# Modulation slices in staging tiles of their own, and 44 stores moved from SP to ACT, in a two-layer hybrid decoder trunk

## The chip, the core and the metric

The kernel runs on one core of a Trainium2 chip. The metric is device time in microseconds: the median over the runs of one kernel. Engines are named as the profile does: PE (TensorE, matrix products and transposes), PEld (its weight loads), DVE (VectorE), ACT (ScalarE), POOL (GpSimd) and SP (SyncE). SP computes nothing here; it is an in-order queue that starts DMA transfers. ACT starts some transfers too, between its own operations. An instruction that waits at the head of an engine's queue holds everything behind it.

## The reference

Two layers over 1024 tokens of width 1024, float32. Each layer:

```
mod = silu(c) @ w_mod + b_mod;  shift, scale, gate = split(mod, 3)
h = rms_norm(x, pre_gain) * (1 + scale) + shift
proj = h @ w_in                      # 1024 x 3088
A: sliding-window attention (window 128, 8 heads, 2 kv heads, rotary, sinks) * silu(ag)
B: rms_norm(retention(rq, rk, rv))  * silu(rg)       # 4 heads, chunks of 128 tokens
C: rms_norm(gated linear attention(gq, gk, gv, log_a)) * silu(gg)
y = concat(A, B, C) @ w_out
x = x + gate * rms_norm(y, post_gain)
```

The modulation is one row of 3 x 1024 values per layer, a product of a vector of 1024 with a 1024 x 3072 matrix.

## The kernel before

**Products.** Tokens are tiled by 128 (t = 0 to 7). A float32 product is made in three passes from a high part (rounded to the format that PE multiplies at full speed) and a low part (the rest). So every weight is loaded as float32, split into a high and a low part, and kept in an arena; activations are split in the same way.

**Weights.** A weight unit is 1024 x 256 (kv, aq0, rq, o0, ...). It comes in four loads of 256 KB (kc = 0 to 3, `issue`, L516), each into one tile of `stage()` (L119, tag `st`, 128 x 512, five buffers, BST). Four conversions (`conv`, L520) make the high parts (line L149 on ACT or L151 on DVE) and four the low parts (L533, three on DVE and one on POOL). A tile of the ring is free for a later load once the low part of its load has been made. The generator `loader` (L474) issues one load, converts one that is two loads old, and yields a delay (`ld1`, `ld2`).

**Modulation.** `mod_third` (L343) makes one third (j = 0 shift, 1 scale, 2 gate) of one layer's modulation in two halves (hh). A half has eight slices of w_mod, 256 KB each (L360), which DVE multiplies by the activated condition and adds up in `acc` (L362, L364). Every slice is put in a tile of `stage()`, the same ring of five as the weight units' loads. So is the row of post-norm gains (L376, L377). Of the 64 slices loaded this way, 16 belong to layer 0 and 48 to layer 1.

**Results of the heads.** Retention (`ret_core`, L1160) works on one token tile at a time: PE transposes the keys (L180), ACT copies them from PSUM (L149), PE makes the scores, DVE applies the causal mask (L1179), and so on; DVE updates the state (L1198, L1200). Gated attention (`gla_core`, L1078) has more steps on DVE, ACT and POOL (L1120, L1121 are its masked scores). `head_norm_gate` (L970) normalises a tile (square on ACT L973, sum on DVE L975, root on POOL L635, products on DVE L978, L979), transposes it, and calls `store_mix` (L954). That makes a high part (L149 on ACT) and a low part (L966 on DVE) and stores both in DRAM (mixS); in the last layer, for tiles 2 and up, a float32 copy as well (mixF). The projection with w_out reads them back.

**What sets the order.** PE's order is written out by hand: a projection emits its matmuls in pieces, and between pieces `pump` (L210) steps the other pieces of work that are due. Each is a generator (a job) that yields a delay from the table `L`, counted on a virtual clock `clk` that matmuls advance by their estimated cost (L164). So a delay decides behind which piece of a projection a small product of attention, retention or modulation stands. A key with `@1` is for layer 1. The order on DVE, ACT, POOL and SP comes from a scheduler that takes the program's instructions by their dependencies, so it moves when the program's order or its tiles move. The table `EN` names the engine of each optional step; `smh` is the store of high parts and of float32 copies, `sml` that of low parts, `lw` the weight loads, `lwm` the slices. `S` is SP and `A` ACT (`dma`, L153).

In the changed kernel all lines from L122 on stand 3 lower: L149 becomes L152, L154 becomes L157, L364 becomes L367.

Of the kernel before, what the change touches and what calls it, by code (L numbers as in the profile page):

```python
# [10 lines left out]
F32 = mybir.dt.float32  # L11
# [6 lines left out]
P = 128  # L18
D = 1024
S = 1024  # L20
# [73 lines left out]
def trunk(ctx: ExitStack, tc: tile.TileContext, ins, cst, out):  # L94
    nc = tc.nc
    V, A, G, T = nc.vector, nc.scalar, nc.gpsimd, nc.tensor
# [6 lines left out]
    gp = ctx.enter_context(tc.tile_pool(name="work", bufs=2))  # L103
# [5 lines left out]
    def nm(s):  # L109
        uid[0] += 1  # L110
        return f"{s}_{uid[0]}"
# [6 lines left out]

    def stage():  # L119
        return gp.tile([P, 512], F32, tag="st", name=nm("st"), bufs=BST)  # L120

    def small(w, dt=F32):  # L122
        return gp.tile([P, w], dt, tag="sm", name=nm("sm"), bufs=BS)
# [4 lines left out]
    def aux(dt=F32):  # L128
        return ps.tile([P, 512], dt, tag="aux", name=nm("aux"), bufs=8 - MMB)
# [14 lines left out]
    def eng(k):  # L144
        return G if EN[k] == "G" else V

    def copy(k, dst, src):
        if EN[k] == "A":
            A.activation(dst, src, AF.Copy)  # L149
        else:  # L150
            V.tensor_copy(dst, src)  # L151

    def dma(k, dst, src):  # L153
        {"S": nc.sync, "A": A, "P": G}[EN[k]].dma_start(dst, src)  # L154

# [8 lines left out]
    def mult(dst, lhsT, rhs, start, stop, cost=None):  # L164
        T.matmul(dst, lhsT, rhs, start=start, stop=stop)  # L165
        if cost is not None:
            clk[0] += cost
            return
        n = 1
        for d in rhs.shape[1:]:  # L170
            n *= d
        c = n / 2400.0
        if rhs.dtype == F32R:
            c = max(c, 0.107 if lhsT.shape[-1] > 64 else 0.055)
        else:
            c = max(4 * c, 0.21 if n > 2 else 0.03)
        clk[0] += c
# [5 lines left out]
    def lat(key, l):  # L183

        return L[key + "@1"] if l and key + "@1" in L else L[key]

# [3 lines left out]
    def flag(name, lat=0.0):  # L190
        flags[name] = clk[0] + lat
# [100 lines left out]
    def mod_tile(l, j):  # L292
        modc[(l, j)] = cp.tile([P, KT], F32, name=nm(f"mod{j}"), tag=f"mod{j}")
# [49 lines left out]
    def mod_third(l, j):  # L343
        if j < 2:
            mod_tile(l, j)
            rows = mod_rows(l, j)
            yield lat("mod1", l)
            rc = mod_rows_t(rows)
        else:
            res = cp.tile([P, D], F32, name=nm("modg"), tag="modg")  # L350
            modg[l] = res
        for hh in range(2):
            c0 = j * D + 512 * hh
            acc = gp.tile([P, 512], F32, tag="acc", name=nm("acc"), bufs=1)
            if j == 2:
                G.memset(acc, 0.0)
                nc.sync.dma_start(acc[0:1, :], b_mod[l:l + 1, c0:c0 + 512])
            for k in range(KT):
                wt = stage()
                dma("lwm", wt, w_mod[l, j, hh, :, k, :])  # L360
                if k == 0 and j < 2:
                    V.tensor_scalar(acc, wt, c_act[:, k:k + 1], None, ALU.mult)  # L362
                else:
                    V.scalar_tensor_tensor(acc, wt, c_act[:, k:k + 1], acc, ALU.mult, ALU.add)  # L364
                yield lat("mod2", l)
            yield lat("mod3", l)
            pm = aux()  # L367
            if j < 2:
                for b in range(4):
                    mult(pm[:, b:b + 1], acc[:, b * P:(b + 1) * P], ones[:, 0:1], True, True)  # L370
                mod_cols(l, j, hh, pm, rc)
                if j == 0:
                    flag(("modh", l, hh), lat("mod4", l))
            else:
                mult(pm, allones, acc, True, True)
                gain = stage()  # L376
# [216 lines left out]
    def sw_second():  # L593
        drain()
        for k in range(4):
# [7 lines left out]
            sw_split("T4", k, s4, "t4")  # L603
            yield L["sw1"]
        for name in ("T2", "T3", "T4"):
# [48 lines left out]
    def pre(l, t, xt, early=False, soon=False):  # L654
# [28 lines left out]
        for j in range(2):  # L683
# [33 lines left out]
    def pre_first(t):  # L717
        xt = [t2(), t2()]
        load_x(t, xt, nc.sync)
        yield L["pf3"] + L["pf2"] * (t - 4)  # L720
        yield from pre(0, t, xt)
# [950 lines left out]
        pump()  # L1672


B2, B1, BS, BST, MMB, SMB = 10, 8, 11, 5, 3, 3
EN = {"shw0": "V", "shw1": "A", "shw2": "A", "shw3": "A", "slw0": "V", "slw1": "G", "slw2": "V", "slw3": "G", "sht2": "A", "sht3": "A", "sht4": "A", "slt2": "V", "slt3": "G", "slt4": "G", "sd": "V", "mh0": "A", "mh1": "A", "mh2": "A", "mh3": "A", "mf": "A", "ms0": "V", "ms1": "V", "ms2": "V", "ms3": "V", "yg0": "V", "yg1": "V", "ml0": "V", "ml1": "V", "ml2": "V", "ml3": "V", "mod0": "A", "mod1": "V", "qst": "S", "smh": "S", "sml": "S", "sm0": "S", "sm1": "S", "lao": "S", "sao": "S", "lmix": "S", "ssg": "S", "lsg": "S", "ssr": "S", "lsr": "S", "lx": "S", "sx": "A", "lw": "S", "lwm": "S", "whi0": "V", "whi1": "A", "whi2": "A", "whi3": "A", "wlo0": "V", "wlo1": "V", "wlo2": "V", "wlo3": "G", "xn0": "V", "xn1": "V", "hlo0": "V", "hlo1": "V", "rot0": "V", "rot1": "V", "rdec": "V", "kslo": "V", "qslo": "V", "vlo": "G", "kT": "A", "qT": "A", "sprev": "A", "pn": "G", "pf0": "A", "aoc": "A", "hng": "V", "mh": "A", "gso": "V", "mg": "V", "mgl": "V", "rT": "A", "rv": "A", "gv": "A", "gk": "A", "ak0": "V", "ak1": "V", "ak2": "V", "ak3": "V", "kd0": "G", "kd1": "G", "kd2": "G", "kx1": "G", "kx2": "G", "kx3": "V", "kx4": "V", "qb": "G", "stx": "V"}
L = {"sw1": 0.4, "ld1": 1.2, "ld2": 1.2, "ld1@1": 1.2, "ld2@1": 1.27, "swW00": 0.0, "swT1": 0.0, "swW11": 0.4, "swW10": 0.5, "tt1": 8.0, "tt2": 1.75, "tb1": 24.5, "tb2": 0.75, "pf3": 13.2, "pf1": 6.35, "pf2": 4.16, "mod1": 4.6, "mod2": 4.0, "mod3": 13.29, "mod4": 7.04, "mod5": 3.36, "mod6": 9.04, "pre1": 7.44, "kv1": 3.1, "kv2": 2.11, "aq1": 6.0, "aq7": 6.0, "ag1": 5.44, "aq2": 2.4, "aq6": 5.2, "aq3": 10.21, "aq4": 7.36, "aq5": 3.6, "hn1": 8.93, "hn2": 2.85, "gz1": 11.18, "gz2": 8.13, "gl1": 2.76, "gd3": 15.9, "gc1": 0.62, "gc2": 1.94, "gc3": 1.33, "gc4": 0.87, "gc6": 0.86, "gc5": 1.14, "rc1": 0.8, "rc2": 1.09, "rc3": 5.87, "rc4": 2.51, "fin1": 7.28, "lay1": 1.13, "gc4@1": 0.93, "mod2@1": 4.0, "mod3@1": 15.1, "mod5@1": 3.36, "mod6@1": 4.11, "pre1@1": 7.44, "kv1@1": 2.79, "kv2@1": 5.28, "aq1@1": 4.8, "aq7@1": 5.28, "ag1@1": 6.25, "aq2@1": 0.82, "aq6@1": 6.0, "aq3@1": 10.9, "aq4@1": 4.4, "aq5@1": 5.15, "hn1@1": 8.12, "hn2@1": 2.85, "gz1@1": 15.91, "gz2@1": 10.94, "gl1@1": 4.6, "gd3@1": 15.9, "gc1@1": 0.48, "gc2@1": 1.94, "gc3@1": 1.33, "gc6@1": 0.86, "gc5@1": 1.04, "rc1@1": 0.37, "rc2@1": 0.84, "rc3@1": 1.9, "rc4@1": 2.79, "fin1@1": 4.28, "lay1@1": 1.7}
CHUNK = 7
LAG = 2
VDB = 8  # L1680
# [41 lines left out]
```

## Time and profile before

| | |
|---|---|
| median of 3 runs | 997.99 us (997.76 to 999.64) |
| the profiled execution | 996.31 us |
| its span | 994.6 us |
| mean granted clock of PE | 0.991 |
| PE busy | 965.7 us, 97% of the span |
| DVE, ACT, POOL busy | 683.2, 409.3, 246.3 us |
| share of PE in the chain that ended last | 80% |
| bytes moved | 148.77 MB |
| modulation slices | 64 loads of 256 KB, median 3.1 us to landing |
| unit loads from w_in | 96 loads of 256 KB, median 3.8 us to landing |

A row of instructions reads: start in us, duration in us, engine, line, operation, written tile <- read tile, shapes, and in brackets the idle time before it with what ended it. A row of waits reads: engine, tile and line of the waiting instruction, what it waited for, then total us, times, longest. A row of the chain reads: start, us, what the end of the kernel hung on at that time. `st` are tiles of the staging ring, `arena` the split weights, `acc` the sum of a modulation half, `t` and `mx` work tiles, `aux` and `mm` PSUM tiles, `SPq` and `ACTq` the engines' queues.

### The profile page before, as it was taken

What the parts mean: (1) busy time and instruction counts of PE and PEld (TensorE: products, weight loads), DVE (VectorE), ACT (ScalarE), POOL (GpSimd) and SP (SyncE); (2) the same over time, 40 slices, a digit from 0 to 9 for tenths busy, and PEclk for the clock granted to TensorE, in tenths of its full rate; (3) what the DMA queues carried; (4) which work ended last, traced back from release to release, by engine and by line L of the source; (5) the groups of instructions that cost most, each with busy time, mean ns of one, the idle gap of its engine ahead of it and who ended that gap; (6) DMA issues with size and microseconds to landing.
All of it is one profiled execution on the core that took longest, in us unless ns stands there. A gap on an engine that the chain in (4) does not pass through costs nothing.

```text
span 994.6 us, 19641 instructions
## 1 busy us (share of the span) xinstructions
PE 965.7 (97%) x7133; PEld 824.3 (83%) x7133; DVE 683.2 (69%) x1679; ACT 409.3 (41%) x1152; POOL 246.3 (25%) x310
## 2 busy tenths in 40 slices
PE   5899999999999999999999999999999999999996
PEld 1599999888998777778889999988999877777785
DVE  3779857677766777664677286775766577567876
ACT  2477312233332656632555332133333257574222
POOL 2322001233310234420124101113322034545000
PEclk8899999999999999999999999999999999999999
DMA  9843513523135355587555241352122434378883
GB/s 321 290 138 97 159 44 115 177 86 121 61 100 166 91 157 168 170 274 239 189 170 171 69 150 38 118 157 83 53 93 86 127 91 133 112 235 266 267 262 139
DMA packets 112305, 148.77 MB, mean 150 GB/s; under 512 B 12065, under 2 KB 63821, under 8 KB 112209
## 3 DMA queue, kind: packets, MB, share of 16 engines
q1 hardware_dynamic: 106512, 137.96, 44.5%
q10 hardware_dynamic: 5696, 9.56, 2.6%
q8 instruction: 56, 0.92, 0.4%
q14 instruction: 41, 0.33, 0.1%
HBM read 109.20 MB, written 36.18 MB: 146 GB/s over the span
## 4 chain that ended last, share of the span: by engine, by line
PE 80%; DVE 7%; DMA 7%; issue 2%; POOL 1%; ACT 1%; SPq 0%; ACTq 0%; POOLq 0%; DVEq 0%
PE mm L165 61%; PE aux L165 14%; PE aux L180 5%; DMA st<-in_w_in_dram 2%; POOL sm L635 1%; DMA t<-aoS 1%; DMA st<-in_w_last_dram 1%; DMA xk<-in_x_dram 1%; DVE arena L533 1%; DMA a<-mixS 1%; DVE t L1248 0%; DVE t L328 0%; DMA t<-in_x_dram 0%; DMA t<-xs 0%; DMA mixS<-t 0%
## 5 line engine op out<-in xcount | busy, mean ns | idle before, releaser
L165 PE MATMUL mm<-arena 128*128 128x256 f32 (+2 forms) x1824 | 299.9, 318 | 1.8 <-ACT arena L704 1.8
L165 PE MATMUL mm<-arena,arena 128*128 128x256 f32 (+2 forms) x1824 | 298.2, 316 | 0.0
L165 PEld LDWEIGHTS mm<-arena 128*128 128x128 f32 x1824 | 255.5, 191 | 26.0 <-issue 3.3
L165 PEld LDWEIGHTS mm<-arena,arena 128*128 128x128 f32 x1824 | 252.2, 188 | 24.3 <-issue 3.7
L635 POOL TENSOR_TENSOR sm<-sm,mhalf 128x1 f32<-128x1 f32 (+1 forms) x64 | 55.8, 872 | 335.9 <-DVE sm L634 317.8
L165 PE MATMUL mm<-arena,mx 128*128 128x512 f32 (+1 forms) x564 | 130.6, 387 | 0.5 <-ACT kept L1341 0.5
L165 PEld LDWEIGHTS mm<-arena,mx 128*128 128x128 f32 x564 | 101.4, 188 | 24.7 <-issue 1.9
L149 ACT ACTIVATE t<-aux 128x256 f32<-128x256 f32 (+2 forms) x124 | 55.8, 468 | 73.8 <-PE aux L180 62.2
L149 ACT ACTIVATE arena<-st 128x512 fp32r<-128x512 f32 x94 | 56.2, 627 | 53.2 <-DMA st<-in_w_in_dram 19.4
L929 POOL TENSOR_TENSOR smx<-smx,sm 128x512 f32<-128x512 f32 x32 | 36.1, 1129 | 125.7 <-DVE sm L928 118.0
L533 POOL TENSOR_TENSOR arena<-st,arena 128x512 fp32r<-128x512 f32 x31 | 42.7, 1378 | 79.7 <-ACT arena L149 72.9
L533 DVE TENSOR_TENSOR arena<-st,arena 128x512 fp32r<-128x512 f32 x77 | 58.0, 775 | 5.2 <-ACT arena L149 3.3
L925 ACT ACTIVATE smx<-smx,sm 128x129 f32<-128x129 f32 x128 | 49.9, 393 | 25.9 <-DVE sm L922 25.7
L364 DVE SCALAR_TENSOR_TENSOR acc<-st,c_act,acc 128x512 f32<-128x512 f32 x60 | 46.7, 778 | 16.9 <-DMA st<-in_w_mod_dram 16.5
L180 PE MATMUL aux<-c_ident,t 128*128 128x128 f32 (+1 forms) x292 | 48.2, 282 | 5.4 <-DVE t L666 5.0
L180 PEld LDWEIGHTS aux<-c_ident,t 128*128 128x128 f32 (+1 forms) x292 | 35.0, 144 | 12.4 <-DVE t L666 6.9
L698 ACT ACTIVATE t<-aux,mod,mod 128x128 f32<-128x128 f32 x68 | 25.9, 459 | 43.0 <-DVE t L1248 18.1
L165 PEld LDWEIGHTS aux<-t,mx 32*128 32x128 f32 (+1 forms) x896 | 39.5, 187 | 3.9 <-issue 2.1
L973 ACT ACTIVATE t<-aux 128x256 f32<-128x256 f32 x32 | 12.3, 383 | 73.6 <-PE aux L165 65.0
L165 PE MATMUL aux<-t,mx 32*128 32x32 f32 (+1 forms) x896 | 40.7, 272 | 0.0
L920 DVE COPY_PREDICATED smx<-c_curmask,aux 128x256 f32<-128x256 int32 x64 | 25.4, 446 | 19.5 <-ACT smx L149 17.2
L1248 DVE SCALAR_TENSOR_TENSOR t<-t,sm,t 128x512 f32<-128x512 f32 x32 | 24.0, 780 | 18.2 <-DMA t<-in_x_dram 10.8
(224 smaller groups left out, 1387.7 us busy)
## 6 DMA issues: line engine op xcount, KB each, us to landing
st<-in_w_in_dram SPq DMA_DIRECT2D x96, 256.0 KB, 3.8
st<-in_w_mod_dram SPq DMA_DIRECT2D x64, 256.0 KB, 3.1
mx<-mixS SPq DMA_DIRECT2D x20, 512.0 KB, 4.9
mixS<-t SPq DMA_DIRECT2D x72, 128.0 KB, 3.7
st<-in_w_last_dram SPq DMA_DIRECT2D x36, 256.0 KB, 3.8
wm<-in_w_mod_dram SPq DMA_DIRECT2D x12, 512.0 KB, 7.0
t<-in_x_dram SPq DMA_DIRECT2D x24, 256.0 KB, 4.9
t<-tabS SPq DMA_DIRECT2D x16, 256.0 KB, 4.6
```

The source lines that it names most:

```text
L149: A.activation(dst, src, AF.Copy)
L165: T.matmul(dst, lhsT, rhs, start=start, stop=stop)
L180: T.transpose(dst, src, idn)
L364: V.scalar_tensor_tensor(acc, wt, c_act[:, k:k + 1], acc, ALU.mult, ALU.add)
L533: e.tensor_tensor(lo, st, f(hi), ALU.subtract)
L635: G.tensor_tensor(r, r, mhalf[:, :w], ALU.pow)
L698: A.activation(hf[:, ks], at[kt], AF.Identity, scale=gain, bias=shift)
L920: V.copy_predicated(sv, curmask.unsqueeze(1).to_broadcast((P, 2, P)), pv[:, :, n // P - 1, :])
L925: A.activation(sm[:, h, :], sm[:, h, :], AF.Exp, bias=mx[:, h:h + 1], accum_out=sums[:, h:h + 1])
L929: eng("pn").tensor_tensor(sm[:, :, 0:128], sm[:, :, 0:128], rs.unsqueeze(2).to_broadcast((P, 4, P)), ALU.mult)
L973: A.activation(sq, po, AF.Square)
L1248: V.scalar_tensor_tensor(xt[j], yg[j], r, xt[j], ALU.mult, ALU.add)
```

## The change

1. `mod_stage()` gives the modulation slices and the gain rows a ring of five tiles of their own (BMOD = 5, 128 x 512 float32). The ring of `stage()` keeps its five and serves the weight loads alone.
2. `smh` goes from `S` to `A`: the 44 stores of high parts (32) and float32 copies (12) of retention and gated attention are started by ACT, which makes these parts. SP starts 596 transfers in place of 640, and ACT 88 in place of 44.
3. Some thirty delays of `L` get other values.
4. The scratch for DMAs that software describes is set to 1024 bytes. The five new tiles take 10 KB of each partition.

No computing instruction is added or left out. Every engine's program is the same up to about 70 us of the profile (SP), 91 (DVE), 97 (ACT, PE) and 240 (POOL).

```
+    def mod_stage():
+        return gp.tile([P, 512], F32, tag="sm8", name=nm("ms"), bufs=BMOD)
...
             for k in range(KT):
-                wt = stage()
+                wt = mod_stage()
                 dma("lwm", wt, w_mod[l, j, hh, :, k, :])
...
                 mult(pm, allones, acc, True, True)
-                gain = stage()
+                gain = mod_stage()
                 nc.sync.dma_start(gain, post_g[l:l + 1, 512 * hh:512 * hh + 512].to_broadcast((P, 512)))
...
-B2, B1, BS, BST, MMB, SMB = 10, 8, 11, 5, 3, 3
+B2, B1, BS, BST, MMB, SMB, BMOD = 10, 8, 11, 5, 3, 3, 5
...
-EN = {... "smh": "S", ...}
+EN = {... "smh": "A", ...}
...
-L = {... "ld1": 1.2, "ld2": 1.2, "tt2": 1.75, "mod3": 13.29, "gd3": 15.9, "gc4": 0.87, "rc4": 2.51, "fin1": 7.28,
-     "mod3@1": 15.1, "kv1@1": 2.79, "gz2@1": 10.94, "gc4@1": 0.93, "gc6@1": 0.86, "rc1@1": 0.37, "rc2@1": 0.84, ...}
+L = {... "ld1": 1.23, "ld2": 0.21, "tt2": 5.32, "mod3": 14.6, "gd3": 11.98, "gc4": 0.0, "rc4": 1.67, "fin1": 6.16,
+     "mod3@1": 14.2, "kv1@1": 3.42, "gz2@1": 14.2, "gc4@1": 1.42, "gc6@1": 0.0, "rc1@1": 1.14, "rc2@1": 2.86, ...}
...
-    nc = _bacc.Bacc("TRN2", target_bir_lowering=False, num_devices=1)
+    nc = _bacc.Bacc("TRN2", target_bir_lowering=False, num_devices=1, dynamic_dma_scratch_size=1024)
```

How this moves instructions, at three places. In these rows a tile's name carries its own number, which differs between the two programs.

ACT at the end of layer 0's retention (190 us in the profile), before: `arena<-st` are weight conversions, `t<-mm` the copy of the values of tile 7, `t<-aux 128x256` the high part of tile 5, and `t<-aux 128x512` the transposed keys of tile 7.

```order
L149 ACTIVATE arena_320<-st_2497 128x512
L149 ACTIVATE arena_320<-st_2509 128x512
L149 ACTIVATE t_418_2442<-mm_2381 128x256
L149 ACTIVATE arena_320<-st_2538 128x512
L149 ACTIVATE t_423_2457<-aux_2454 128x256
L149 ACTIVATE t_427_2472<-aux_2467 128x512
```

The same place in the changed kernel:

```order
L152 ACTIVATE arena_320<-st_2484 128x512
L152 ACTIVATE arena_320<-st_2501 128x512
L152 ACTIVATE arena_320<-st_2513 128x512
L152 ACTIVATE t_419_2446<-mm_2385 128x256
L152 ACTIVATE t_421_2451<-aux_2448 128x256
L157 DMA mixS<-t_421_2451 128x256
L152 ACTIVATE t_428_2476<-aux_2471 128x512
```

The third conversion has gone ahead of the copy of the values, and the store of the high part stands between the two copies from aux.

SP at the end of layer 1's retention (655 to 666 us), before: `st<-in_w_in` are loads of weight units, `st<-in_w_mod` the last slice of the modulation, `mixF` and `mixS` the stores of retention tile 5, and `t<-srS` the gate row for a retention tile.

```order
L154 DMA st_8316<-in_w_in_dram 128x512
L154 DMA st_8329<-in_w_mod_dram 128x512
L154 DMA mixF<-t_1455_8232 128x256
L154 DMA mixS<-t_1456_8235 128x256
L154 DMA st_8334<-in_w_in_dram 128x512
L154 DMA mixS<-t_1457_8236 128x256
L154 DMA st_8363<-in_w_in_dram 128x512
L154 DMA st_8380<-in_w_in_dram 128x512
L154 DMA st_8392<-in_w_in_dram 128x512
L154 DMA t_1480_8349<-srS 128x256
```

The changed kernel, from the last two slices (`ms`) on:

```order
L157 DMA ms_8287<-in_w_mod_dram 128x512
L157 DMA ms_8337<-in_w_mod_dram 128x512
L380 DMA ms_8583<-in_post_norm_gain_dram 128x512
L157 DMA mixS<-t_1403_7942 128x256
L157 DMA t_1419_8046<-srS 128x256
L157 DMA st_8248<-in_w_in_dram 128x512
L157 DMA t_1434_8118<-srS 128x256
L157 DMA st_8278<-in_w_in_dram 128x512
L157 DMA st_8307<-in_w_in_dram 128x512
L157 DMA st_8324<-in_w_in_dram 128x512
L157 DMA st_8342<-in_w_in_dram 128x512
L157 DMA mixS<-t_1448_8184 128x256
```

The slices and the gain row have gone ahead of the unit loads, two retention tiles earlier; of a tile's three stores one, the low part, is left on SP.

ACT at the same place of the changed kernel, with what each instruction waits for (`PE`, `DVE`, `Activation`: that engine's work; `DMAHW` with a number: one of the counters by which SP's and ACT's transfers report that they have landed):

```order
L152 ACTIVATE t_1447_8183<-aux_8177 128x256 [waits DVE_49]
L157 DMA mixF<-t_1446_8180 128x256 [waits DMAHW7_49,Activation_49]
L157 DMA mixS<-t_1447_8183 128x256 [waits DMAHW1_49,Activation_49]
L152 ACTIVATE t_1455_8236<-mm_8204 128x256 [waits DMAHW7_49,PE_49]
L152 ACTIVATE arena_320<-st_8342 128x512 [waits DMAHW0_49,PE_49]
L152 ACTIVATE t_1459_8262<-aux_8257 128x512 [waits PE_49]
```

Before, the same copies stood there without the two stores, which were on SP. Both stores now wait for a transfer's counter besides their own copy; over the program 23 of the 44 do.

More of the change, by code (lines that the diff above doesn't have):

```diff
@@ L1677 @@
-L = {"sw1": 0.4, "ld1": 1.2, "ld2": 1.2, "ld1@1": 1.2, "ld2@1": 1.27, "swW00": 0.0, "swT1": 0.0, "swW11": 0.4, "swW10": 0.5, "tt1": 8.0, "tt2": 1.75, "tb1": 24.5, "tb2": 0.75, "pf3": 13.2, "pf1": 6.35, "pf2": 4.16, "mod1": 4.6, "mod2": 4.0, "mod3": 13.29, "mod4": 7.04, "mod5": 3.36, "mod6": 9.04, "pre1": 7.44, "kv1": 3.1, "kv2": 2.11, "aq1": 6.0, "aq7": 6.0, "ag1": 5.44, "aq2": 2.4, "aq6": 5.2, "aq3": 10.21, "aq4": 7.36, "aq5": 3.6, "hn1": 8.93, "hn2": 2.85, "gz1": 11.18, "gz2": 8.13, "gl1": 2.76, "gd3": 15.9, "gc1": 0.62, "gc2": 1.94, "gc3": 1.33, "gc4": 0.87, "gc6": 0.86, "gc5": 1.14, "rc1": 0.8, "rc2": 1.09, "rc3": 5.87, "rc4": 2.51, "fin1": 7.28, "lay1": 1.13, "gc4@1": 0.93, "mod2@1": 4.0, "mod3@1": 15.1, "mod5@1": 3.36, "mod6@1": 4.11, "pre1@1": 7.44, "kv1@1": 2.79, "kv2@1": 5.28, "aq1@1": 4.8, "aq7@1": 5.28, "ag1@1": 6.25, "aq2@1": 0.82, "aq6@1": 6.0, "aq3@1": 10.9, "aq4@1": 4.4, "aq5@1": 5.15, "hn1@1": 8.12, "hn2@1": 2.85, "gz1@1": 15.91, "gz2@1": 10.94, "gl1@1": 4.6, "gd3@1": 15.9, "gc1@1": 0.48, "gc2@1": 1.94, "gc3@1": 1.33, "gc6@1": 0.86, "gc5@1": 1.04, "rc1@1": 0.37, "rc2@1": 0.84, "rc3@1": 1.9, "rc4@1": 2.79, "fin1@1": 4.28, "lay1@1": 1.7}
+B2, B1, BS, BST, MMB, SMB, BMOD = 10, 8, 11, 5, 3, 3, 5
@@ new lines @@
+EN = {"shw0": "V", "shw1": "A", "shw2": "A", "shw3": "A", "slw0": "V", "slw1": "G", "slw2": "V", "slw3": "G", "sht2": "A", "sht3": "A", "sht4": "A", "slt2": "V", "slt3": "G", "slt4": "G", "sd": "V", "mh0": "A", "mh1": "A", "mh2": "A", "mh3": "A", "mf": "A", "ms0": "V", "ms1": "V", "ms2": "V", "ms3": "V", "yg0": "V", "yg1": "V", "ml0": "V", "ml1": "V", "ml2": "V", "ml3": "V", "mod0": "A", "mod1": "V", "qst": "S", "smh": "A", "sml": "S", "sm0": "S", "sm1": "S", "lao": "S", "sao": "S", "lmix": "S", "ssg": "S", "lsg": "S", "ssr": "S", "lsr": "S", "lx": "S", "sx": "A", "lw": "S", "lwm": "S", "whi0": "V", "whi1": "A", "whi2": "A", "whi3": "A", "wlo0": "V", "wlo1": "V", "wlo2": "V", "wlo3": "G", "xn0": "V", "xn1": "V", "hlo0": "V", "hlo1": "V", "rot0": "V", "rot1": "V", "rdec": "V", "kslo": "V", "qslo": "V", "vlo": "G", "kT": "A", "qT": "A", "sprev": "A", "pn": "G", "pf0": "A", "aoc": "A", "hng": "V", "mh": "A", "gso": "V", "mg": "V", "mgl": "V", "rT": "A", "rv": "A", "gv": "A", "gk": "A", "ak0": "V", "ak1": "V", "ak2": "V", "ak3": "V", "kd0": "G", "kd1": "G", "kd2": "G", "kx1": "G", "kx2": "G", "kx3": "V", "kx4": "V", "qb": "G", "stx": "V"}
@@ new lines @@
+L = {"sw1": 0.4, "ld1": 1.23, "ld2": 0.21, "ld1@1": 1.2, "ld2@1": 1.27, "swW00": 0.0, "swT1": 0.0, "swW11": 0.4, "swW10": 0.5, "tt1": 8.6, "tt2": 5.32, "tb1": 24.5, "tb2": 0.75, "pf3": 13.2, "pf1": 6.35, "pf2": 4.23, "mod1": 4.6, "mod2": 4.0, "mod3": 14.6, "mod4": 7.04, "mod5": 3.36, "mod6": 8.16, "pre1": 7.44, "kv1": 3.1, "kv2": 2.11, "aq1": 6.0, "aq7": 6.0, "ag1": 5.92, "aq2": 2.4, "aq6": 5.2, "aq3": 10.21, "aq4": 7.36, "aq5": 3.6, "hn1": 8.93, "hn2": 2.77, "gz1": 11.18, "gz2": 8.13, "gl1": 2.76, "gd3": 11.98, "gc1": 0.62, "gc2": 1.94, "gc3": 1.33, "gc4": 0.0, "gc6": 0.86, "gc5": 1.14, "rc1": 0.8, "rc2": 1.09, "rc3": 5.87, "rc4": 1.67, "fin1": 6.16, "lay1": 0.83, "gc4@1": 1.42, "mod2@1": 4.0, "mod3@1": 14.2, "mod5@1": 3.36, "mod6@1": 4.11, "pre1@1": 7.44, "kv1@1": 3.42, "kv2@1": 5.28, "aq1@1": 4.8, "aq7@1": 5.28, "ag1@1": 7.65, "aq2@1": 0.82, "aq6@1": 6.49, "aq3@1": 10.9, "aq4@1": 4.25, "aq5@1": 5.15, "hn1@1": 8.22, "hn2@1": 2.85, "gz1@1": 15.91, "gz2@1": 14.2, "gl1@1": 4.6, "gd3@1": 15.9, "gc1@1": 0.52, "gc2@1": 1.82, "gc3@1": 1.33, "gc6@1": 0.0, "gc5@1": 1.04, "rc1@1": 1.14, "rc2@1": 2.86, "rc3@1": 1.9, "rc4@1": 2.79, "fin1@1": 4.28, "lay1@1": 1.62}
```

1 line of the change is left out of this document (removed).

## The prediction

> **What bounds the kernel now.** The page's first part comes first, then busy time cut into stretches.
>
> ```profile
> PE 965.7 (97%) x7133; PEld 824.3 (83%) x7133; DVE 683.2 (69%) x1679; ACT 409.3 (41%) x1152; POOL 246.3 (25%) x310
> 25.00:175.00 150.00, 146.51 (x1162) 137.21 (x1161) 118.42 (x314) 68.16 (x165) 29.07 (x39) 0.98 0.44 141
> 175.00:200.00 25.00, 23.71 (x175) 21.50 (x174) 16.72 (x47) 7.51 (x16) 6.53 (x5) 1.00 0.55 166
> 225.00:275.00 50.00, 49.41 (x607) 45.52 (x606) 37.11 (x120) 17.87 (x56) 18.39 (x26) 1.00 0.31 95
> 525.00:550.00 25.00, 24.86 (x204) 24.64 (x203) 16.84 (x40) 13.52 (x41) 7.95 (x17) 1.00 0.51 161
> 650.00:675.00 25.00, 22.58 (x173) 20.57 (x173) 18.86 (x50) 7.27 (x16) 6.23 (x5) 1.00 0.62 184
> 725.00:750.00 25.00, 24.84 (x298) 23.66 (x295) 17.10 (x61) 9.53 (x31) 8.84 (x13) 1.00 0.23 76
> 925.00:950.00 25.00, 23.01 (x98) 18.04 (x97) 20.34 (x39) 8.22 (x17) 2.17 (x3) 1.00 0.84 261
> 975.00:994.60 19.60, 11.62 (x63) 9.75 (x61) 11.87 (x24) 3.08 (x10) 1.47 (x2) 0.91 0.32 115
> ```
>
> The columns are the stretch, its length, busy time of PE, PEld, DVE, ACT and POOL, the granted clock, the DMA share and GB/s. PE is busy in 97% of the span at clock 1.00, and the change gives it no matmul more or less. So the whole gain has to come out of PE's idle time, and that is small. The start is the same program up to about 70 us, so what PE lacks there (and most of the 3.5 us in 25 to 175) stays; the end after the last matmul stays too. What is left is 25.00 - 23.71 = 1.29 us at 175 to 200, 0.59 at 225 to 275, 0.14 at 525, **2.42 at 650 to 675**, 0.16 at 725 and **1.99 at 925 to 950**: 6.6 us in all, 0.66% of the span. That is the ceiling of this change.
>
> **Who ends these waits.** At 187 to 193 (retention of the first layer), ACT's and PE's rows:
>
> ```profile
> 189.35 0.63 ACT L149 ACTIVATE arena<-st 128x512 fp32r<-128x512 f32 x1 [1.72 <-DMA st<-in_w_in_dram]
> 191.39 0.63 ACT L149 ACTIVATE arena<-st 128x512 fp32r<-128x512 f32 x1 [1.14 <-DMA st<-in_w_in_dram]
> 191.93 0.85 ACT L149 ACTIVATE t<-aux 128x256 fp32r<-128x256 f32 x2
> 188.84 0.82 PE L180 MATMUL aux<-c_ident,t 128*128 128x128 f32 x6
> 189.41 2.13 PE L165 MATMUL mm<-arena,arena 128*128 128x512 f32 x8
> 192.83 0.71 PE L165 MATMUL aux<-t 64*128 64x128 f32 x8 [1.29 <-ACT t L149]
> ```
>
> PE waits 1.29 us for the copy of the transposed keys, the second of the two copies at 191.93. Its input was there when the transposes ended, 188.84 + 0.82 = 189.66. The copy was late because a weight conversion ahead of it in ACT's queue stood until 191.39 for its load.
>
> At 655 to 675 (the same place in layer 1): PE's waits, ACT's, and the chain.
>
> ```profile
> PE aux L165 <- ACT t L149: 1.8, 2, 1.2
> PE aux L165 <- DVE t L1179: 0.4, 1, 0.4
> ACT arena L149 <- DMA st<-in_w_in_dram: 9.9, 5, 3.7
> 656.79 0.66 DVE acc L364
> 657.48 3.52 DMA st<-in_w_in_dram
> 662.95 3.42 DMA st<-in_w_in_dram
> 666.86 0.70 DVE arena L533
> 667.58 3.61 DMA st<-in_w_in_dram
> ```
>
> Here the shared ring of five tiles is seen directly. The load of 657.48 starts when a modulation product (acc, L364) has read its slice out of the tile that the load needs. ACT then stands 9.9 us in five waits for such loads, and PE 1.8 us behind ACT.
>
> At 240 to 258 (gated attention), ACT's copy of a high part, and the chain that its store makes:
>
> ```profile
> 240.86 0.42 ACT L149 ACTIVATE t<-aux 128x256 fp32r<-128x256 f32 x1
> 240.43 1.75 POOL arena L533
> 242.20 0.33 SPq L154
> 242.63 3.24 DMA mixS<-t
> 245.97 0.39 ACT t L973
> 257.37 0.33 PE aux L180
> ```
>
> SP holds a weight load until POOL has freed its tile; the high-part store stands behind it and goes at 242.63, and ACT's square (L973) waits for the tile that the store reads. Through the norm and DVE this ends in PE at 257.37.
>
> At the end (last output):
>
> ```profile
> 897.10 0.37 SPq L154
> 897.51 2.88 DMA st<-in_w_last_dram
> 937.16 7.31 DMA a<-mixS
> 944.61 11.50 PE mm L165 x48
> ```
>
> PE's wait there is for a load of 7.31 us in a stretch with a DMA share of 0.84: bytes, as much as order.
>
> **The change part by part.**
>
> *Own tiles for the slices.* No instruction is added: 64 slice loads, 4 gain loads and 64 products go on as before. The unit loads now cycle through five tiles alone, so they are issued when a conversion five loads back is done, and no more behind a product such as the one at 656.79. In the changed order SP has the last slices of the third modulation part ahead of all the unit loads that were late. In layer 0 the copy of the keys would then be done at 189.66 + 0.85 (the two copies of 191.93) + 0.37 (a store that now stands between them, priced below) = 190.9, before PE asks at 189.41 + 2.13 = 191.54. The whole 1.29 goes if the loads are early, and nothing if the conversions, of which three now stand ahead of the copy, are as late as before. I take **1.0** (0 to 1.3).
>
> In layer 1 I take **1.9 of 2.42**: what remains is one conversion of 0.63 us left in the way, less 0.1. DVE's 18.86 busy of 25 there lose two products of about 0.7 each, which helps L1179 and L1200. Bounds 0 and 2.4.
>
> *Stores from ACT.* PE's waits for ACT's copies over the whole span, SP's issues of such stores, and a store's and a load's time to landing:
>
> ```profile
> PE aux L165 <- ACT t L149: 3.0, 3, 1.3
> L154 SPq DMA_DIRECT2D mixS<-t x96: 319/366/958, 134.2 to 933.1; - x96
> mixS<-t SPq DMA_DIRECT2D x72, 128.0 KB, 3.7
> st<-in_w_in_dram SPq DMA_DIRECT2D x96, 256.0 KB, 3.8
> ```
>
> The 44 issues (32 of high parts, 12 of float32) cost SP a median of 0.366 us, 16.1 us in sum, and about that on ACT. ACT is idle for 994.6 - 409.3 = 585 us, so nearly all is covered. Where it is not, the next instruction in ACT's queue is 0.37 late. The order shows a copy for the retention scores right behind a store six times; without cover that is 6 x 0.37 = 2.2 us. All 44 uncovered would be 16.1. By the first row (PE waits for ACT's copies three times in the span) most have cover: I take **0.3 lost**, with 0 and 2.2 as ends, since the other stores are followed by copies of results that PE doesn't ask for at once. The gain: a high part goes as soon as its copy is done. At 242 the copy ended at 240.86 + 0.42 = 241.28 and the store left at 242.63, so 1.35 of the chain go; the delay gc4, set from 0.87 to 0, brings PE's question nearer by up to 0.87. I take **0.4 gained** of the 0.59 there, with -0.9 and +0.6 as ends.
>
> The Trainium skill weighs against this part: "DMA: Bandwidth & Descriptors", section "Issuing engines are not separate DMA queues", says that starting transfers from several engines saves only the sequencer's time of starting them, usually little beside the transfer. The rows of 240.43 to 245.97 show something else besides, a store held by the load ahead of it on an in-order queue. By the rule alone the 0.4 would be nothing, and the forecast 0.4 higher.
>
> *Delays.* They move PE's small groups between pieces of the projections. The PE rows are the same in number and kind, so this part is worth what it does to waits. At 525 and 725 (0.14 and 0.16) I take **0.1**. At the end, the two weight loads that stood behind the store of 897.10 now go ahead of it. Against that stands the 0.84 of DMA share, which no reordering lowers. I take **0.7 of 1.99** (0 to 2.0). What new waits the delays make no row can show; the nearest, the largest wait that one retention tile makes here, is 1.3, and I leave it to the range.
>
> *The smaller scratch* changes no instruction and is taken as nothing: the kernel starts no DMA from POOL.
>
> **Sum.** 1.0 + 1.9 + 0.4 + 0.7 + 0.1 - 0.3 = 3.8 us. Against the profiled execution (996.31, a span of 994.6 and 1.7 around it) this gives 992.5. The median of the runs shown, 997.99, is 1.68 above that execution, so as a median I expect 997.99 - 3.8 = **994.2**. About 0.2%, 2 us, is what a measurement of this kernel can tell from no change.
>
> **Rivals.**
>
> *1. The next dependency takes over.* In both retention ends three weight conversions still stand ahead of the copy, and in layer 1 the conversions of DVE stand ahead of the causal products that PE needs. If only the load's lateness shrinks and the conversions still land in front of the copies, I count 0.4 of 1.29, 0.9 of 2.42 and nothing at the end: 1.3, less 0.8 for stores and new waits, 0.5. Time 997.5. For it: the load of 667.58 follows a conversion (666.86, L533), not a product. Against it: the chain that this conversion is part of begins with the product of 656.79.
>
> *2. ACT is held by its own stores: slower.* DMAs of SP and ACT share the counters that say when a transfer has landed, and in the changed order 23 of the 44 stores wait for such a counter besides their copy, mostly one used by a load of SP. If that load was issued late, the store stands, and behind it ACT's whole queue: the copies for PE. One late case holds ACT up to 3.8 us (the load's landing), less the 0.6 that the copy has at 190.9 against 191.54, so about 3; it decides as soon as a load is issued less than 3.8 us ahead of the store that shares its counter, and the loads at 655 to 675 stand that close. Three such cases make 9, less the 3.8: time about 1003; two make about 1000. For it: this queue was clear of such waits before, with the copies of PE in it, and 6 stores stand right ahead of one. Against it: by their places in the present trace most of these transfers are landed well before the store, and with tiles of their own the loads will be earlier still.
>
> *3. All of it goes.* The ceiling, 6.6, and no loss: 991.4.
>
> DVE's waits for the slices themselves are a smaller doubt of the second rival's sign:
>
> ```profile
> DVE acc L364 <- DMA st<-in_w_mod_dram: 16.5, 13, 3.7
> ```
>
> DVE stands 16.5 us for slices, 13 times. In the changed order the products stand earlier and closer together; with five tiles of their own I count these waits as no longer than now.
>
> **How the numbers follow.** Forecast and third rival, 991.2 to 995.9: 0.60. First rival, 996 to 1000: 0.17. Second, above 1000: 0.23. The two signs hold most of the chance, so the likeliest case's own range is 991.2 to 995.9. The range over all reaches from 991.2 to 1001.5, which leaves out the upper part of the second rival and a little beyond the ceiling, under 0.2 in all. Faster by over 0.2% (below 996.0): 0.60; within: 0.17; slower: 0.23.
>
> **What the changed profile would show.** If right: PE idle under 0.4 us in the first retention end (near 190 us) and under 0.8 in that of layer 1; no wait of a unit load for a modulation product in the chain; ACT's waits for unit loads there well under the 9.9; the store at the gated attention issued on ACT within half a microsecond of its copy; the load of a from mixS at the end still some 6 to 7 us. The first rival would show these loads early, and PE waiting for DVE (L533's products, causal products) in the same places. The second would show ACT's queue standing at a DMA with a landing of SP's load behind it, and PE waits for L149 copies in more than three places. The forecast is wrong if PE's idle time between 70 and 985 us is not under 4 us.

## The result, and the profile after

| | before | changed |
|---|---|---|
| median (range, runs) | 997.46 us (994.87 to 1001.68, 22) | 995.41 us (992.12 to 999.90, 22) |
| ratio, 95% interval | | 0.9977 (0.9966 to 0.9988) |
| profiled execution, span | 996.31, 994.6 us | 992.12, 990.4 us |

By the ratio the changed kernel is faster by 0.23%, 2.3 us (1.2 to 3.4); the medians differ by 2.05. The forecast was 3.8. The two profiled executions differ by 4.2: the changed kernel's is the fastest of its 22 runs, 3.3 below their median, and that of before is 1.2 below its own. Where PE's idle time went is read from the busy time by stretch, with the columns of the prediction (length of the stretch, then PE's busy time, whose difference is PE's idle time); first before from 70 to 980 us (the last matmul of both kernels ends later), then the changed kernel:

```profile
70.00:980.00 910.00, 903.41 (x6787) 779.47 (x6786) 631.40 (x1556) 373.25 (x1056) 223.70 (x272) 1.00 0.46 142
```

```profile
70.00:980.00 910.00, 907.43 (x6808) 783.29 (x6807) 633.24 (x1559) 373.60 (x1057) 221.84 (x272) 1.00 0.45 142
175.00:200.00 25.00, 24.45 (x182) 22.24 (x180) 15.88 (x45) 7.53 (x16) 5.79 (x5) 1.00 0.46 143
225.00:275.00 50.00, 49.72 (x617) 46.19 (x616) 35.37 (x117) 18.20 (x60) 17.59 (x26) 1.00 0.27 86
275.00:525.00 250.00, 249.72 (x1473) 199.10 (x1472) 172.76 (x373) 116.59 (x351) 62.41 (x73) 1.00 0.57 178
650.00:675.00 25.00, 25.00 (x186) 22.84 (x185) 18.24 (x50) 8.34 (x19) 5.48 (x5) 1.00 0.56 174
725.00:750.00 25.00, 24.41 (x334) 23.12 (x333) 17.32 (x62) 10.53 (x36) 7.96 (x12) 1.00 0.31 97
925.00:950.00 25.00, 24.51 (x105) 19.16 (x104) 20.70 (x41) 8.43 (x20) 1.50 (x2) 1.00 0.85 274
```

PE's idle time between 70 and 980 us falls from 6.59 to 2.57 us. The 2.42 of layer 1's retention end are gone altogether, 1.29 at 175 to 200 became 0.55, 0.59 at 225 to 275 became 0.28, 1.99 near the end 0.49. What grew is 0.59 (0.16 before) at 725 to 750, and 0.28 at 275 to 525, 0.21 at 675 to 725 and 0.16 at 70 to 175, where there was none.

At layer 0's retention end the old chain is still there, weaker. ACT's rows and PE's of the changed kernel:

```profile
189.45 0.63 ACT L152 ACTIVATE arena<-st 128x512 fp32r<-128x512 f32 x1 [1.21 <-DMA st<-in_w_in_dram]
189.99 0.36 ACT L152 ACTIVATE t<-mm 128x256 f32<-128x256 f32 x1
190.25 0.38 ACT L152 ACTIVATE t<-aux 128x256 fp32r<-128x256 f32 x1
190.66 0.33 ACTq L157 DMA_DIRECT2D mixS<-t  x1
191.08 0.60 ACT L152 ACTIVATE t<-aux 128x512 f32<-128x512 f32 x1 [0.46 <-DMA st<-in_w_in_dram]
191.73 0.71 PE L168 MATMUL aux<-t 64*128 64x128 f32 x8 [0.55 <-ACT t L152]
```

A conversion still waits 1.21 us for its load, and the store at 190.66 stands between the two copies. In this order the store adds 0.4 to PE's wait of 0.55. In layer 1, ACT's waits for unit loads are 4.1 us (9.9 before), and at the gated attention a store goes right behind its copy:

```profile
ACT arena L152 <- DMA st<-in_w_in_dram: 4.1, 3, 2.4
```

```profile
238.04 0.38 ACT L152 ACTIVATE t<-aux 128x256 fp32r<-128x256 f32 x1
238.45 0.36 ACTq L157 DMA_DIRECT2D mixS<-t  x1
```

### The profile page after: what moved, and what is told of

It reads as the page before. It is cut to its first block, busy times and chain, and to the rows that moved or that the text cites. A ratio compares the mean times of both kernels' runs of the same rounds, so it can differ in the third digit from the quotient of the medians.

```text
span 990.4 us, 19626 instructions
## 1 busy us (share of the span) xinstructions
PE 964.5 (97%) x7133; PEld 824.7 (83%) x7133; DVE 683.3 (69%) x1679; ACT 409.5 (41%) x1152; POOL 244.7 (25%) x310
## 5 line engine op out<-in xcount | busy, mean ns | idle before, releaser
L536 DVE TENSOR_TENSOR arena<-st,arena 128x512 fp32r<-128x512 f32 x77 | 61.6, 821 | 2.9 <-ACT arena L152 1.6
L367 DVE SCALAR_TENSOR_TENSOR acc<-ms,c_act,acc 128x512 f32<-128x512 f32 x60 | 45.6, 759 | 5.3 <-DMA ms<-in_w_mod_dram 4.4
```

The source lines that it names most:

```text
L536: e.tensor_tensor(lo, st, f(hi), ALU.subtract)
```

## The experiments

Twelve kernels, each timed in five rounds against the kernel before on the same chip; two chips were used, so a ratio is always to the runs of before on its own chip. The first seven are the parts of the change, their pairs, and the whole once more. "Idle" time is PE's.

| own tiles | stores on ACT | new delays | ratio (95% interval) |
|---|---|---|---|
| yes | | | 1.0104 (1.0086 to 1.0121) |
| | yes | | 1.0016 (1.0002 to 1.0030) |
| | | yes | 1.0051 (1.0036 to 1.0066) |
| yes | yes | | 1.0025 (1.0005 to 1.0046) |
| | yes | yes | 1.0055 (1.0036 to 1.0074) |
| yes | | yes | 0.9972 (0.9960 to 0.9983) |
| yes | yes | yes | 0.9974 (0.9962 to 0.9987) |

### Own tiles alone

```
-                wt = stage()
+                wt = mod_stage()          # gain rows too, and the smaller scratch; "smh": "S" and the old L kept
```

> Only the five tiles of their own for the slices (and the smaller scratch); stores on SP and delays as before. The prediction's theory (own tiles carry the gain): PE's idle time at 650 to 675 falls from 2.42 us to under 0.8 and at 175 to 200 from 1.29 to under 0.6, no unit load follows a modulation product in the chain, the time falls by 2 to 3 us (ratio 0.997 to 0.998). Rival, the delays carry it: the two retention ends keep more than two thirds of their idle time (over 1.6 and over 0.9 us), since the loads are issued when the jobs' delays say so, and the time stays within 1 us of before.

Measured: 1.0104, 10 us slower; both theories are out. Layer 1's retention end, first in stretches of 4 us (the column before the last two is the granted clock), then the chain there:

```profile
670.00:674.00 4.00, 3.78 (x25) 3.07 (x25) 1.00 (x2) 0.22 (x1) 0.02 (x1) 1.00 0.57 176
674.00:678.00 4.00, 1.94 (x14) 1.71 (x14) 1.96 (x4) 1.52 (x4) 0.00 (x0) 1.00 0.93 267
678.00:682.00 4.00, 3.04 (x13) 2.43 (x14) 2.38 (x8) 1.18 (x3) 2.28 (x2) 0.53 0.61 212
682.00:686.00 4.00, 4.00 (x16) 3.28 (x15) 0.54 (x2) 0.00 (x0) 0.00 (x0) 0.62 0.15 39
```

```profile
672.17 0.65 SPq L157
672.87 4.84 DMA st<-in_w_in_dram
678.33 0.59 ACT t L152
678.96 1.23 PE aux L168 x8
```

The unit load no longer stands behind a modulation product, but it is as late as before: it goes at 672.87, behind SP's other issues, and the key copy waits for its conversion. Just ahead of it SP issues three stores of results (671.23 to 672.82). PE idles 3.2 us between 670 and 682, and at 678.2 its clock is halved: the trace's clock record has 6.83 us at one half there and 3.41 near 224, so 10.24 us at half speed cost up to 5.1. Another wait is new:

```profile
PE aux L183 <- DVE t L669: 2.9, 1, 2.9
```

It is near 506 us, where layer 1 begins: its normed input is late. The chain there starts with a load of x of 6.6 us that lands at 498.8, and goes on over DVE's work, a modulation product of 0.67 us among it. 5.1 + 2.9 and the growth of the retention end, about 1.2, make 9.2 of the 10.8 us between the spans.

### Stores alone

```
-"smh": "S"
+"smh": "A"
```

> Only the 44 stores of high and float32 parts on ACT; one shared ring of five tiles and the old delays. The prediction's theory: worth about nothing, 0.1 us faster by its sum (0.4 gained at the gated attention, 0.3 lost behind stores); the retention ends keep their 2.4 and 1.3 us. Rival, ACT held by its stores: PE waits for ACT's copies (L149) in more than three places, over 3.0 us in sum, and the time is 1 us or more above before.

Measured: 1.0016, 1.6 us slower (0.2 to 3.0), where 0.1 faster was expected. The rival's sum and time came, its "more than three places" did not: PE waits for ACT's copies 4.2 us in three places, as many as before (3.0 us). The largest growth, 1.29 to 2.1, is at layer 0's retention end. ACT's rows there, and PE's wait:

```profile
191.18 1.32 ACT L149 ACTIVATE arena<-st 128x512 fp32r<-128x512 f32 x2 [2.91 <-DMA st<-in_w_in_dram]
193.08 0.33 ACTq L154 DMA_DIRECT2D mixS<-t  x1
193.45 0.60 ACT L149 ACTIVATE t<-aux 128x512 f32<-128x512 f32 x1 [0.40 <-ACT t L149]
```

```profile
PE aux L165 <- ACT t L149: 2.1, 1, 2.1
```

The load is late, and the store adds its 0.4 to a copy that is late already; that is half of the growth of 0.8. So the stores cost where the cover is gone, at the price that the prediction gave them. At the gated attention, where they were to gain 0.4, they gain nothing; these are the stretch with the stores alone and with the delays alone (next experiment):

```profile
225.00:275.00 50.00, 49.41 (x578) 45.62 (x577) 38.25 (x123) 17.76 (x55) 19.12 (x30) 1.00 0.30 94
225.00:275.00 50.00, 49.77 (x581) 46.29 (x581) 38.87 (x123) 17.15 (x55) 18.46 (x28) 1.00 0.29 91
```

The 0.59 us of idle time of before is still there with the stores, and is 0.23 with the delays.

### Delays alone

```
-L = {... "ld2": 1.2, "tt2": 1.75, ...}
+L = {... "ld2": 0.21, "tt2": 5.32, ...}    # all 28
```

> Only the new delays; shared ring and stores on SP as before. The prediction's theory: 0.5 to 1 us faster (the end of the program and small waits), the retention end of layer 1 keeps over 1.6 of its 2.42 us. Rival, the delays carry it: the time falls by 2 us or more and the retention ends lose most of their idle time without tiles of their own. A third: the delays were set for the ring of ten and cost 1 us or more without it.

Measured: 1.0051, 5.1 us slower: the third reading. Layer 1's retention end did lose half of its idle time (1.25 of 2.42 left), but see the clock behind it:

```profile
690.00:694.00 4.00, 3.98 (x22) 2.68 (x20) 3.39 (x10) 1.47 (x5) 0.00 (x0) 1.00 0.33 104
694.00:698.00 4.00, 3.83 (x57) 3.37 (x58) 1.01 (x5) 1.20 (x6) 0.00 (x0) 0.83 0.31 98
698.00:702.00 4.00, 4.00 (x59) 3.29 (x57) 0.00 (x0) 0.00 (x0) 0.71 (x3) 0.50 0.03 6
702.00:706.00 4.00, 4.00 (x18) 3.61 (x15) 3.60 (x9) 1.34 (x6) 1.72 (x4) 0.50 0.00 0
```

10.24 us at half clock cost some 5.1 us, most of the 6.2 between the spans. It begins at 696.7 with no wait over 0.2 us beside it, at the first small products (32 x 32) of the gated attention. So the third reading came out in size; that the smaller ring sets the clock off is not shown.

### The changed kernel once more

> The changed kernel itself once more, for a second profile. If the stretches of PE's idle time are a property of the program, they come back within 0.3 us each: under 0.8 at 175 to 200, under 0.3 at 650 to 675, under 0.8 at 925 to 950. If they hang on how the transfers fell in one execution, one of them is 1 us or more off.

Measured: 0.9974, and nearly the same picture: 0.70 us idle at 175 to 200, none at 650 to 675, 0.82 at 925 to 950. The last is 0.33 off and a little over its bound, and no stretch up to 975 us is 1 us off. So the idle time is in the main a property of the program.

```profile
70.00:980.00 910.00, 907.06 (x6806) 783.11 (x6805) 633.24 (x1561) 374.44 (x1060) 223.53 (x272) 1.00 0.46 142
```

The first profile has 907.43 where this line has 907.06.

### Tiles and delays, stores on SP

```
-"smh": "A"
+"smh": "S"                                # else the changed kernel
```

> Own tiles and new delays; the 44 stores back on SP. PE's order is that of the changed kernel. Theory after the single parts (tiles and delays only pay together, the stores pay nothing): ratio 0.996 to 0.9985, PE idle in both retention ends under 0.8 us in sum, no stretch at half clock between 60 and 985 us. Rival, the stores are the third leg: the store of high parts is held on SP again, retention or gated attention lose over 1 us more than in the changed kernel, or a stretch at half clock appears, ratio 1.000 or more.

Measured: 0.9972, with 0.75 and 0.12 us idle at the two retention ends and no half clock in between.

```profile
175.00:200.00 25.00, 24.25 (x179) 21.98 (x179) 16.18 (x46) 7.52 (x16) 5.79 (x5) 1.00 0.49 148
650.00:675.00 25.00, 24.88 (x188) 22.82 (x187) 18.55 (x51) 8.22 (x19) 5.07 (x4) 1.00 0.56 175
70.00:980.00 910.00, 905.68 (x6793) 780.91 (x6793) 632.62 (x1558) 372.28 (x1057) 223.72 (x272) 1.00 0.46 142
```

The sum at the two ends, 0.87, is just over the 0.8 expected. By the times the stores pay nothing here: the gain is that of tiles and delays together, each of which alone is a loss. But each interval is 1.2 us to either side, and PE idles 4.3 us between 70 and 980 us here, against 2.6 and 2.9 in the two profiles with the stores on ACT, so a gain of 1 us by the stores is not ruled out. At layer 0's retention end PE's wait is no shorter without the store between the copies (0.75): here the copy of the high part waits 0.51 us for an earlier store to leave its tile.

### Tiles and stores with the old delays

```
-L = {... new ...}
+L = {... of before ...}                   # else the changed kernel
```

> Own tiles and stores on ACT with the old delays. PE's order is that of before. If the old delays are what makes own tiles slow, this is as slow as the tiles alone: ratio 1.007 to 1.012, with PE's wait of some 3 us near 506 us and the idle time at 670 to 682 us of the tiles alone. If the stores held on SP make the late loads there, the retention end of layer 1 loses that idle time and the ratio is under 1.005.

Measured: 1.0025, between the two. PE waits 2.0 us at layer 1's start and 1.2 at its retention end, and two stretches of 3.41 us run at half clock. So the old delays make own tiles a loss (PE's order is that of before in both), but three quarters of the 10 us went with the stores, which are all that differs from the tiles alone. With SP free of them the retention end of layer 1 lost two thirds of its idle time (1.2 of 3.7 us left) and its half clock; that the three stores at 671 to 673 us were what held the load there is the reading that fits, and no run tries these three by themselves.

### Delays and stores with the shared ring

> New delays and stores on ACT with the shared ring of five. If the shared ring is what the new delays don't bear, the ratio is that of the delays alone, 1.003 to 1.008, again with PE at half clock for about 10 us after the retention end of layer 1. If the stores decide, it is at or under 1.000.

Measured: 1.0055, as the delays alone. The half clock is elsewhere than expected, from 198.0 us for 3.41 us, after a wait of 2.6 us for ACT's key copy:

```profile
186.00:196.00 10.00, 8.17 (x59) 6.97 (x58) 7.71 (x18) 3.81 (x8) 0.92 (x2) 1.00 0.67 206
196.00:200.00 4.00, 3.24 (x15) 2.58 (x16) 0.92 (x3) 0.60 (x1) 0.50 (x1) 0.76 0.64 199
```

### One ring of ten

```
-        return gp.tile([P, 512], F32, tag="sm8", name=nm("ms"), bufs=BMOD)
+        return gp.tile([P, 512], F32, tag="st", name=nm("ms"), bufs=BST)      # BST = 10
```

> The changed kernel with one shared ring of ten tiles in place of two rings of five: the same memory, delays and stores. If the number of tiles is what counts, this is like the changed kernel (0.996 to 0.999, retention ends under 0.8 us of PE idle time in sum). If the separation counts (a unit load doesn't stand behind a modulation product), unit loads follow products again and the ratio is above 0.999, with idle time of 1 us or more at a retention end.

Measured: 1.0024 (1.0007 to 1.0042). As many tiles do not do it. (The ring `st` serves not only weight loads, in any version: ACT's squares at L1352 and L1452 and reloaded results at L1315 take tiles of it too.) Idle time is 1.32 us at 650 to 675 and 2.72 at 525 to 550. In the chain of the latter DVE stands for a slice, and everything of layer 1 behind it:

```profile
531.55 0.67 DVE acc L367
532.23 4.66 DMA ms<-in_w_mod_dram
536.99 0.75 DVE acc L367
```

So in one ring it is here the slices that come late, the other way round than the theory had it for 650 us of the kernel before. Some 1.7 us of the loss are another 3.41 us at half clock, from 697 us.

### Which delays

```
-L = {...}
+L = {... the 14 changed keys with "@1" as before ...}      # first kernel
+L = {... the 14 changed keys without "@1" as before ...}   # second kernel
```

> The changed kernel with the 14 changed delays of layer 1 set back to those of before. Theory: own tiles need the layer's own delays; the late loads and PE's waits at the retention end of layer 1 (650 to 690 us) come back, over 1 us of idle time there, while the wait near 506 us of the tiles alone stays away; ratio 1.000 to 1.005. Rival, the delays of layer 0 suffice: ratio 0.996 to 0.999 and under 0.5 us idle there.

Measured: 1.0019 (1.0001 to 1.0036). As the theory had it: a wait of 1.3 us is back in layer 1, and none near 506.

```profile
650.00:675.00 25.00, 23.69 (x176) 21.62 (x175) 16.99 (x46) 7.94 (x18) 7.30 (x6) 1.00 0.55 169
```

```profile
PE aux L168 <- DVE t L1182: 1.3, 1, 1.3
```

This kernel's profiled execution was its fastest, 992.86 us, as fast as the changed kernel's; its median is 999.17 and its slowest run 1003.16. Over its twelve runs the mean granted clock goes from 0.992 to 0.984, and the time with it. One profile alone would have called this kernel a success.

> The changed kernel with the 14 other changed delays (those without a layer: layer 0 and the loader) set back. Theory: PE's wait of 2 to 3 us near 506 us, at the start of layer 1, comes back, and a half clock near 222 us may; the retention end of layer 1 stays under 0.5 us idle; ratio 1.000 to 1.005. Rival, the delays of layer 1 suffice: ratio 0.996 to 0.999.

Measured: 1.0050 (1.0027 to 1.0072), again as the theory had it: PE's wait at the start of layer 1 is back, the retention end of layer 1 is clear (25.00 of 25.00 busy). The half clock comes three times, one of them in that wait:

```profile
PE aux L183 <- DVE t L669: 2.4, 1, 2.4
```

```profile
495.00:498.00 3.00, 1.01 (x5) 1.04 (x6) 2.87 (x8) 0.00 (x0) 0.55 (x1) 0.82 0.50 179
498.00:501.00 3.00, 3.00 (x12) 2.57 (x11) 2.06 (x6) 1.91 (x5) 0.55 (x1) 0.61 0.25 87
```

So own tiles need the new delays of both layers: those without a layer for the start of layer 1, those of layer 1 for its retention end.

### Twice the stores on ACT

```
-"sml": "S"
+"sml": "A"
```

> The changed kernel with the stores of low parts on ACT as well, so ACT's issues double. If a store on ACT costs little (0.3 us per 44 by the prediction), nothing is to be seen: ratio 0.996 to 0.999, PE's waits for ACT's copies L152 under 1.2 us in sum. If ACT's queue is held by stores that wait (DVE makes the low parts, so ACT waits for DVE there), PE waits for copies of ACT over 3 us in sum and the ratio is over 1.000.

Measured: 0.9988 (0.9975 to 1.0001), inside the first band, and no slower than before. PE's wait for ACT's copies is at the bound:

```profile
PE aux L168 <- ACT t L152: 1.2, 1, 1.2
PE mm L168 <- ACT kept L1344: 2.1, 1, 2.1
PE mm L168 <- DVE t L1348: 2.0, 1, 2.0
```

The other two lines are at the end of the program, at 930 and 953 us, and new in their size (before, 0.5 us for the one, and the other is not listed). With the one at 930, another copy by ACT, the sum is 3.3, over the other reading's 3 us, though the ratio is not over its 1.000; the last store that this edit gives to ACT goes at 775.5 us, so neither wait is behind one. The edit raises these stores from 44 to 76. This profile is of the slowest of the kernel's twelve runs.

### Three tiles for the slices

```
-BMOD = 5
+BMOD = 3
```

> The changed kernel with three tiles of their own for the slices in place of five. If all that counts is that unit loads stand behind no product, three do as well: ratio 0.996 to 0.999 and under 0.8 us idle at the two retention ends together. If the delays fit this one order alone, a ring of three gives another order and loses: ratio over 0.999, with waits of over 1 us somewhere between 175 and 975 us.

Measured: 1.0000 (0.9978 to 1.0022), which settles nothing: the median is 1.6 us below that of before, three runs of eleven are 2 to 9 us above it. Idle time at the retention ends is 0.68 and 0 us, the largest wait 1.0 us near the end.

## Why the prediction was right, and where not

**The bound** was right: nothing but PE's idle time between 70 and 980 us could go, and 4.0 of 6.6 us went. The sign of being wrong that the prediction set itself, 4 us or more of idle time between 70 and 985 us, was badly cut: 985 lies behind the last matmul of the changed kernel (981.9), so it reads 5.68 there; up to 980 it is 2.57. Of its signs, layer 1's retention end (0 us idle), ACT's waits for loads (4.1 for 9.9), the store at the gated attention and the load of `a` (6.4 us) came as said. Layer 0's retention end did not: 0.55 and 0.70 us in the two profiles, where under 0.4 was asked.

**The terms**, against the profile: 1.0 was 0.74 at layer 0's retention end, 1.9 was 2.42 at layer 1's, 0.4 was 0.31 at the gated attention, 0.7 was 1.50 at the end. The 0.1 for the rest was a loss of 0.9 (0.59 against 0.16 at 725, where layer 1's gated attention now waits, 0.28, 0.21 and 0.16 in stretches that had none, and 0.14 gained at 525). The sum is 4.0 against 3.8, but by luck in part: 0.8 too little at the end and 1.0 too much for the rest cancel. That the spans differ by about as much, 4.2, is chance too: outside 70 to 980 us some 1.0 more is idle at the start and after the last matmul, and PE's busy time is 1.2 shorter (964.5 for 965.7).

**The attribution** was wrong. The prediction gave 2.9 of its 3.8 us to the tiles as such, by the step "the unit loads ... are issued when a conversion five loads back is done, and no more behind a product". No late load stands behind such a product any more, but with the tiles alone the late one stands behind a conversion and three stores, and the tiles alone lose 10 us. When a conversion is made is set by the loader's and the jobs' delays, and DVE's products go where the new order puts them; the delays of before, kept, put both in places where PE waits. That mechanism is argued from the kernel's text; what the runs show is that the pair gains and each part alone loses. The delays, which got 0.8 in the sum, lose alone too, 5 us, and without them the tiles gain nothing. Tiles and delays cannot be valued one at a time, so 2.9 as the worth of the tiles was wrong. That the idle time at the two retention ends fell by about as much, 3.2, is the work of both.

**The stores** were taken as 0.4 gained and 0.3 lost. In the changed kernel nothing of either is to be seen in the time (0.9972 without them, 0.9974 with); a copy that is late already they hold up by 0.4. In the pair with the old delays they mattered far more than that, 8 us, which the sum did not see. By the rule of the Trainium skill, "DMA: Bandwidth & Descriptors", section "Issuing engines are not separate DMA queues", they were to bring nothing, and the 0.4 at the gated attention were the prediction's addition. The store does go 0.03 us behind its copy (238.45 against 238.04 + 0.38), but the 0.31 us gained there need no store on ACT: the stores alone leave the 0.59, the delays alone make it 0.23, and so do tiles and delays without the stores (tiles and stores with the old delays leave 0.34). For that place the rule's value stands. The 8 us with the old delays are more than it lets expect; by the reading above, a store that is off SP no longer holds the loads behind it.

**The size of the median.** The profiled executions differ by 4.2 us, the medians by 2.05. The prediction put the median 1.68 above the profile for both kernels; it is 1.2 above it before and 3.3 in the changed kernel. The granted clock goes with that difference. Of 34 runs of the changed kernel 15 had a mean clock of 0.991 or more; their median is 993.7. The other 19 have 996.5. Before, in the runs beside the experiments: 997.2 (48 runs) and 998.1 (37). At the higher clock the gain is 3.5 us, near the forecast; at the lower 1.6. The prediction took PE's clock of 1.00 from one profile as given. That the clock is the missing term fits these medians, but is not shown place by place: both profiles of the changed kernel are of runs at the higher clock.

**The rivals.** ACT held by its own stores did not come with own tiles and the new delays, with 44 stores or with 76. The next dependency took over in part at layer 0's retention end, for 0.55 us.

## What to carry to other kernels

Where an order is written out by hand with delays, the delays are fitted to the buffers: a buffer that removes a wait can lose more than the wait until the delays are set again, so try the parts in pairs before a gain is put down to one of them. On a kernel that keeps PE 97% busy the idle time by stretch gives the ceiling, and the granted clock of many runs, not one profile, gives what of it arrives. An issue that moves to another queue is worth what it holds up, which was nothing to be seen with the new delays and 8 us with the old.

## What the runs showed of the hardware that had not been expected

PE's clock fell to one half in the middle of the program in the profiles of seven of the twelve experiments, eleven times in all, for lengths of 3.41, 6.83 and 10.24 us, that is one, two and three times 3.41. Within a profile the falls also begin whole multiples of 3.41 us apart: with the old delays of layer 0 at 223.85, 496.91 and 950.89 us, 80 and 133 times. So the profiles can be cut into windows of 3.41 us on each one's own grid, and a fall begins where a window ends. Three such windows, the first two of the tiles alone, the third of tiles and stores:

```profile
504.12:507.54 3.42, 1.80 (x8) 1.13 (x6) 3.42 (x10) 3.15 (x9) 0.13 (x1) 1.00 0.86 281
507.54:510.95 3.41, 2.10 (x14) 1.88 (x15) 2.97 (x7) 2.10 (x8) 0.73 (x1) 1.00 0.72 253
503.08:506.50 3.42, 1.45 (x8) 0.88 (x7) 2.97 (x10) 2.28 (x7) 0.87 (x1) 1.00 0.97 293
```

The longest wait of all, 2.93 us at 506 us in the tiles alone, is followed by no fall: it lies in two windows, with 1.62 and 1.31 us of idle time. The wait of 1.97 us at the same place in the third row lies in one, and there the clock falls, at 506.5. Over all fourteen profiles, from 60 to 975 us, the five windows with the most idle time (1.97 to 2.38 us) are each followed by a fall. Of the others, which idle 1.62 us or less, one with 1.48 is followed by the fall at 678.2, and those that idle more than it by none. So in these runs a fall goes with the idle time within one window, and not with the length of a wait; where the bound lies is not sharp.

The other five falls begin with no wait over 0.2 us, at 224 and 697 us, each behind a window that holds a whole group of 56 products of 32 x 32 of the gated attention. At full clock 126 windows hold such a group; the seven of them with the longest time without any larger product (2.16 to 2.37 us) include these five, and two that no fall follows (2.20 and 2.22). That many small products are to the clock much like idle time is a reading that fits; no run here tried it by itself.

The Trainium skill, "TensorE: Matmul & The Clock Gate", section "HAM oscillation — how this bites in real kernels", says to allow no idle gap of PE over some 3.4 us. The lengths here agree with the window that the page gives, but five falls followed single waits of 2.0 to 2.6 us, so the bound measured here is lower. The kernel before idles 2.42 us at 650 to 675, in several waits of which the longest is 1.22, and kept its clock in the profile.
